# Two tiles of an encoder kernel grow by 32 bytes, and the tiles behind them move in SBUF

## The chip, the core and the metric

The kernel runs on one core of a Trainium2 chip. The metric is the device time of one execution in microseconds (us). Three runs of the kernel before took 1504.77, 1505.03 and 1505.45 us.

## The reference

One encoder layer on 256 tokens of width 2048, float32: an rmsnorm, a combined input projection, windowed and dilated attention, two gated branch projections, an output projection, a gated MLP with a depthwise convolution of width 3, and a gated per-layer embedding. Cut to its products:

```python
proj = rms_norm(x, attn_norm) @ w_in                 # q, k, v, two gates
ya, yb = windowed_gqa(...), dilated_attention(...)
merged = sigmoid(ga) * (ya @ w_branch_a) + sigmoid(gb) * (yb @ w_branch_b)
x = x + merged @ w_out
hf = rms_norm(x, ffn_norm)
x = x + (gelu(dwconv(hf @ w_ffn_gate)) * (hf @ w_ffn_up)) @ w_ffn_down
x = x + sigmoid(rms_norm(x, ple_norm) @ w_ple_gate) * (p @ w_ple_proj)
return rms_norm(x, final_norm)
```

## The kernel before

Tokens lie along the free dimension and features on the 128 partitions. Every weight matrix is cut into blocks of 128x128, and all blocks come in one stream, in the order in which they are used: `load` (L168) brings 16 blocks at a time (1 MB) into one of three `raw` tiles, and `split_to` (L178) turns 8 blocks at a time into two tiles, `whi` (L187, ScalarE, rounded to float32r) and `wlo` (L188, VectorE, the remainder). The activations are split in the same way: a tile such as `mov` holds 256 columns of high parts and then 256 of low parts for each of its 16 chunks of features.

A product takes two matmuls for each block (`block`, L192): the high weights are the stationary operand for 512 moving columns (L198), and the low weights for the 256 high columns (L199). This text calls the two a **pair**. 64 pairs at the start write `first`, and 3552 write `acc`. Two other forms take three matmuls for a step: `value_product` (L241, lines L253 to L255) with 256 moving columns, and `wide_product` (L211, lines L220 to L222) with 512. In these two forms the weights are the moving operand and the activations (`mov`, or `pw`) the stationary one.

The order of the work is written out in `_plan` (L62) as a list of jobs, and TensorE follows it:

- the keys, queries and values, with attention between them: `scores` and `values` (three matmuls, L435 to L437, on `kf`, `qf`, `near` and `v`), and transposes against `ident` (L489);
- 16 rounds of gates and branches: two gates of 16 pairs each from `mov`, then a branch of 8 and one of 4 pairs from `yab`; the first two rounds have gates alone, and two rounds of branches alone end the stage;
- the output projection (16 jobs of 16 pairs from `mov`, kind `o`);
- twice: gates and ups of the MLP (kinds `g` and `u`, 44 jobs of 16 pairs from `mov`), then its down product (kinds `d0` and `d1`, 16 jobs of 22 pairs from `act`). Between the jobs of `d1` the residual is transposed (L638);
- the embedding: `wide_product` on `pw` (kind `pp`, 8 steps) and on `mov` (kind `pg`, 64 steps).

Tiles come from pools that are laid one behind another in SBUF, each tile padded to a multiple of 32 bytes per partition. So a tile's place follows from the sizes ahead of it. The pool `const` (L136) holds `x`, `cl`, `ident`, `ones`, `mhalf` and `warm`; behind it lie `wpool` (`raw`, `whi`, `wlo`), `big` (the two tiles `mov`), `sc` (`tot`, `tb`, `sq`, `t` and others), and then `att`, or later `ff`. `cl` takes 992 bytes, which is 32 bytes more than a multiple of 64, and so what stands behind it is 32 bytes off a multiple of 64; `warm` (16 bytes padded to 32) sets the place of `wpool` and `big`, and `tb` (80 bytes padded to 96) that of all that comes after it. In the programs the places, modulo 64 bytes, are:

| tiles | before | after |
|---|---|---|
| `x`, `cl` | 0 | 0 |
| `ident`, `ones` | 32 | 32 |
| `raw`, `whi`, `wlo` | 32 | 0 |
| `mov` (both), `tot` | 32 | 0 |
| `t`, `u`, `sq`, `rms` and the other wide tiles of `sc` | 0 | 0 |
| `yab`, `near`, `s`, `k`, `kf`, `q`, `qf`, `v`, `vf`, `far` | 0 | 0 |
| `act`, `pw`, `ph`, `c`, `gw` | 0 | 0 |

The slices that the matmuls read start at multiples of 512 bytes within their tiles, so each operand has its tile's remainder. (`value_product` also reads every second token of `mov`, which starts 0 or 4 bytes further on.)

Of the kernel before, what the change touches and what calls it, by code (L numbers as in the profile page):

```python
# [10 lines left out]
F32 = mybir.dt.float32  # L11
FR = mybir.dt.float32r
AF = mybir.ActivationFunctionType
# [3 lines left out]
P = 128  # L17
# [10 lines left out]
NH = QH + BH  # L28
NBUCK = 32
# [103 lines left out]
def _encoder(ctx: ExitStack, tc, xt, pt, cols, table, onehot, mask, ident_in, last_gain, wts, out):  # L133
    nc = tc.nc

    const = ctx.enter_context(tc.tile_pool(name="const", bufs=1))  # L136
# [10 lines left out]
    nc.vector.memset(ones, 1.0)  # L147
    mhalf = const.tile([P, 4], F32, name="mhalf")
    nc.vector.memset(mhalf, -0.5)
    warm = const.tile([P, 4], F32, name="warm")  # L150
    nc.scalar.activation(warm, mhalf, AF.Tanh)
    idle = ps.tile([P, P], F32, name="misc")
    for _ in range(WARM):
        nc.tensor.matmul(idle, ones, ones, start=True, stop=True)
# [106 lines left out]
    sc = ctx.enter_context(tc.tile_pool(name="sc", bufs=2))  # L261
# [95 lines left out]
    hba = hb[:, :QH * AW].rearrange("p (h c) -> p h c", c=AW)  # L357
    hbb = hb[:, QH * AW:].rearrange("p (h c) -> p h c", c=BW)
    oh = ap_.tile([NBUCK, 2 * T], F32, name="oh", tag="near", bufs=1)
    tb = sc.tile([NBUCK, NH], F32, name="tb", bufs=1)  # L360
    mk = ap_.tile([NH, 2 * T], F32, name="mk", tag="s1", bufs=2)
    squares = ap_.tile([P, 4, T], F32, name="squares", tag="s3", bufs=1)

# [427 lines left out]
```

## Time and profile before

| what | value |
|---|---|
| median of three runs | 1505.03 us |
| the profiled execution | 1504.69 us |
| its span in the profile | 1502.9 us |
| VectorE busy | 1051.7 us (70%) |
| ScalarE busy | 765.6 us (51%) |
| DMA, mean | 187 GB/s |

The span runs from the first to the last instruction in the profile; the other 1.8 us of the execution lie around it. In a group of instructions "x2656" is their count and the last number before the bar is the mean duration of one. Matmuls overlap, so the duration of one (394 ns for 512 columns) is longer than the time from one start to the next, which is what sets the pace. In the windows, "(x694)" counts the instructions that touch a stretch of time.

### The profile page before, as it was taken

To read this page: it belongs to the slowest core of one execution; us is meant where nothing else is said; L and a number is where in the kernel's file an instruction comes from. 1 tells how busy PE (TensorE), PEld (TensorE's weight loads), DVE (VectorE), ACT (ScalarE), POOL (GpSimd) and SP (SyncE) were. 2 spreads that over 40 slices of the span, in tenths; PEclk is the share of its full clock that TensorE was granted. 3 is DMA by queue.
4 is the path that set the end of the run, shared out by engine and by line. 5 is a ranking of instruction groups with operands and counts; after the bars stand their busy time and mean duration, and the time that the engine had idled before them with its cause. 6 is when DMAs were issued, how large, how long until landed. Compare 5 with 4: busy or idle time off the path is not lost.

```text
span 1502.9 us, 22107 instructions
## 1 busy us (share of the span) xinstructions
PE 1487.2 (99%) x8680; PEld 1307.7 (87%) x8680; DVE 1051.7 (70%) x1626; ACT 765.6 (51%) x1179; POOL 33.1 (2%) x36
## 2 busy tenths in 40 slices
PE   9999999999999999999999999999999999999996
PEld 7999999988888888888888888888888888888885
DVE  8786665666666677678888885557888887656564
ACT  6564444445555555554555554444555555555543
POOL 7000000000000000000000000000000000000000
PEclk9999999999999999999999999999999999999999
DMA  7744455445555555565555555555555555555552
GB/s 263 278 141 169 168 172 186 160 170 184 194 196 180 188 194 191 182 222 182 186 193 196 188 181 192 196 182 184 195 196 185 184 192 196 176 189 174 190 196 84
DMA packets 43651, 280.95 MB, mean 187 GB/s; under 512 B 4820, under 2 KB 7892, under 8 KB 10908
## 3 DMA queue, kind: packets, MB, share of 16 engines
q1 hardware_dynamic: 42972, 277.45, 52.4%
q10 hardware_dynamic: 576, 2.10, 0.4%
q8 instruction: 68, 1.11, 0.3%
q14 instruction: 35, 0.29, 0.1%
HBM read 277.39 MB, written 2.14 MB: 186 GB/s over the span
## 4 chain that ended last, share of the span: by engine, by line
PE 97%; DVE 1%; DMA 1%; issue 0%; SPq 0%; ACT 0%; DVEq 0%; POOLq 0%; POOL 0%; ACTq 0%
PE acc L198 55%; PE acc L199 28%; PE acc L220 2%; PE acc L222 2%; PE acc L221 2%; PE acc L253 2%; PE acc L255 2%; PE acc L254 2%; DMA raw<-in_wts 1%; PE pt L489 0%; DVE mov L285 0%; DVE wlo L188 0%; PE misc L638 0%; PE misc L504 0%; PE sp L454 0%
## 5 line engine op out<-in xcount | busy, mean ns | idle before, releaser
L198 PE MATMUL acc<-mov,whi 128*128 128x512 f32 x2656 | 928.5, 394 | 0.0
L188 DVE TENSOR_TENSOR wlo<-raw,whi 128x1024 fp32r<-128x1024 f32 (+1 forms) x517 | 635.9, 1230 | 405.4 <-ACT whi L187 405.1
L187 ACT ACTIVATE whi<-raw 128x1024 fp32r<-128x1024 f32 (+1 forms) x517 | 547.3, 1059 | 642.7 <-PE acc L198 390.6
L199 PE MATMUL acc<-mov,wlo 128*128 128x256 f32 x2656 | 741.7, 279 | 0.0
L198 PEld LDWEIGHTS acc<-mov,whi 128*128 128x128 f32 x2656 | 497.6, 187 | 112.2 <-DVE mov L280 0.3
L199 PEld LDWEIGHTS acc<-mov,wlo 128*128 128x128 f32 x2656 | 500.9, 189 | 0.1
L198 PE MATMUL acc<-act,whi 128*128 128x512 f32 x704 | 247.5, 394 | 0.0
L199 PE MATMUL acc<-act,wlo 128*128 128x256 f32 x704 | 196.5, 279 | 0.0
L198 PEld LDWEIGHTS acc<-act,whi 128*128 128x128 f32 x704 | 131.9, 187 | 31.3
L199 PEld LDWEIGHTS acc<-act,wlo 128*128 128x128 f32 x704 | 132.0, 187 | 0.0
L268 ACT ACTIVATE t<-acc 128x256 f32<-128x256 f32 x230 | 84.2, 369 | 22.9 <-PE acc L199 22.9
L272 DVE TENSOR_TENSOR u<-acc,t 128x256 f32<-128x256 f32 x197 | 81.5, 417 | 2.1 <-ACT t L268 2.1
L198 PE MATMUL acc<-yab,whi 128*128 128x512 f32 x192 | 68.4, 396 | 0.0
L253 PE MATMUL acc<-whi,mov 128*128 128x256 f32 x224 | 63.5, 284 | 0.0
L255 PE MATMUL acc<-whi,mov 128*128 128x256 f32 x224 | 63.4, 283 | 0.0
L254 PE MATMUL acc<-wlo,mov 128*128 128x256 f32 x224 | 63.3, 283 | 0.0
L199 PE MATMUL acc<-yab,wlo 128*128 128x256 f32 x192 | 53.9, 281 | 0.0
L220 PE MATMUL acc<-whi,mov 128*128 128x512 f32 x128 | 49.9, 390 | 0.0
L222 PE MATMUL acc<-whi,mov 128*128 128x512 f32 x128 | 49.8, 389 | 0.0
L221 PE MATMUL acc<-wlo,mov 128*128 128x512 f32 x128 | 49.8, 389 | 0.0
L253 PEld LDWEIGHTS acc<-whi,mov 128*128 128x128 f32 x224 | 43.3, 194 | 1.1 <-ACT whi L187 0.8
L198 PEld LDWEIGHTS acc<-yab,whi 128*128 128x128 f32 x192 | 36.0, 188 | 8.8
(143 smaller groups left out, 1034.3 us busy)
## 6 DMA issues: line engine op xcount, KB each, us to landing
raw<-in_wts SPq DMA_DIRECT2D x254, 1024.0 KB, 4.8
raw<-in_wts SPq DMA_DIRECT2D x7, 512.0 KB, 8.1
x<-in_xt SPq DMA_DIRECT2D x7, 256.0 KB, 7.6
mov<-hold SPq DMA_DIRECT2D x3, 514.0 KB, 7.6
mov<-hold SPq DMA_DIRECT2D x2, 768.0 KB, 7.1
mov<-in_last_gain ACTq DMA_DIRECT2D x1, 1024.0 KB
out<-mov SPq DMA_DIRECT2D x2, 384.0 KB, 2.5
out<-mov ACTq DMA_DIRECT2D x2, 384.0 KB, 3.2
```

Of the source, the lines that this page charges most:

```text
L187: nc.scalar.activation(hi, src, AF.Copy)
L188: nc.vector.tensor_tensor(lo, src, hi.bitcast(F32), op=ALU.subtract)
L198: nc.tensor.matmul(acc, hi[:, o, :], m, start=first, stop=False, skip_group_check=True)
L199: nc.tensor.matmul(acc[:, T:], lo[:, o, :], m[:, :T], start=False, stop=last, skip_group_check=True)
L220: nc.tensor.matmul(accs[t], xh, hi, start=(k == 0), stop=False)
L221: nc.tensor.matmul(accs[t], xh, lo, start=False, stop=False)
L222: nc.tensor.matmul(accs[t], xl, hi, start=False, stop=(k == n - 1))
L253: nc.tensor.matmul(acc[:, :T], xh, hi, start=(k == 0), stop=False)
L254: nc.tensor.matmul(acc[:, :T], xh, lo, start=False, stop=False)
L255: nc.tensor.matmul(acc[:, :T], xl, hi, start=False, stop=(k == KC - 1))
L268: keep(nc.scalar.activation(t, acc[:, T:], AF.Copy, scale=scale))
L272: nc.vector.tensor_tensor(u, acc[:, :T], t, op=ALU.add)
```

## The change

`warm` gets 12 columns in place of 4, of which the same four are written. `tb` gets 28 columns in place of 20, of which the same 20 are used. Both tiles take 32 bytes more per partition, so `wpool` and `big` move by 32 bytes, and what lies behind `tb` by 64. Every instruction is the same on every engine, in the same order and with the same waits; only addresses differ.

```diff
-    warm = const.tile([P, 4], F32, name="warm")
-    nc.scalar.activation(warm, mhalf, AF.Tanh)
+    warm = const.tile([P, 12], F32, name="warm")
+    nc.scalar.activation(warm[:, :4], mhalf, AF.Tanh)
...
-    tb = sc.tile([NBUCK, NH], F32, name="tb", bufs=1)
+    tb = sc.tile([NBUCK, NH + 8], F32, name="tb", bufs=1)[:, :NH]
```

## The prediction, made before the run

> **What bounds the kernel now.** I read the first page first, for the engine that is never idle, and then the chain of work that ended last.
>
> ```profile
> span 1502.9 us, 22107 instructions
> PE 1487.2 (99%) x8680; PEld 1307.7 (87%) x8680; DVE 1051.7 (70%) x1626; ACT 765.6 (51%) x1179; POOL 33.1 (2%) x36
> PEclk9999999999999999999999999999999999999999
> PE 97%; DVE 1%; DMA 1%; issue 0%; SPq 0%; ACT 0%; DVEq 0%; POOLq 0%; POOL 0%; ACTq 0%
> L198 PE MATMUL acc<-mov,whi 128*128 128x512 f32 x2656 | 928.5, 394 | 0.0
> L199 PE MATMUL acc<-mov,wlo 128*128 128x256 f32 x2656 | 741.7, 279 | 0.0
> L198 PE MATMUL acc<-act,whi 128*128 128x512 f32 x704 | 247.5, 394 | 0.0
> L198 PE MATMUL acc<-yab,whi 128*128 128x512 f32 x192 | 68.4, 396 | 0.0
> L220 PE MATMUL acc<-whi,mov 128*128 128x512 f32 x128 | 49.9, 390 | 0.0
> ```
>
> TensorE is 99% busy, its clock is at full speed in every slice, and 97% of the chain is its own work: the end is set by how closely matmuls follow each other. The mean durations say nothing of that (394 ns from `mov` and from `act` alike), because matmuls overlap. So I counted matmuls in long stretches that hold nothing but pairs of one kind: the output projection (from `mov`), the first gates and ups (`mov`), the first down product (`act`), the second gates and ups (`mov`).
>
> ```profile
> core 0: us, PE busy (x), PEclk, DMA share, GB/s
> 899.00:1019.00 120.00, 120.00 (x688) 1.00 0.53 185
> 1025.00:1145.00 120.00, 120.00 (x694) 1.00 0.54 191
> ...
> 700.00:820.00 120.00, 120.00 (x694) 1.00 0.54 191
> 568.00:652.00 84.00, 84.00 (x477) 1.00 0.54 190
> ```
>
> A count takes in matmuls already under way (0.33 us of them, about the mean duration of one), so the time of a pair is twice (stretch + 0.33) / count. That gives 346.8 ns for gates and ups, **349.8 ns from `act`**, and 353.6 ns in the output projection, though all four have the same shapes, the same engine clock and no idle time. There are three rhythms here. `mov` is read in two of them, so it has a good one and a bad one; `act` has one in between. (A pair has 768 columns.) By the table of places, `mov` with `whi` and `wlo` are all at 32 modulo 64, while `act` is at 0 and its weights at 32.
>
> The embedding product shows the same more sharply, in two jobs that take turns. Both stream the same weights tile (at 32); the stationary operand is `pw` (at 0) or `mov` (at 32).
>
> ```profile
> 1401.47 0.40 PE L221 MATMUL acc<-wlo,pw 128*128 128x512 f32 x1
> ...
> 1403.82 0.40 PE L222 MATMUL acc<-whi,pw 128*128 128x512 f32 x1
> ...
> 1404.28 0.39 PE L220 MATMUL acc<-whi,mov 128*128 128x512 f32 x1
> ...
> 1405.87 0.39 PE L221 MATMUL acc<-wlo,mov 128*128 128x512 f32 x1
> ```
>
> From `pw`, ten matmuls lie between the two starts: 2.35 / 10 = 235 ns each. From `mov` there are seven: 1.59 / 7 = 227 ns. So the pace is lower where the two operands of a matmul have different remainders, whichever of them is at 0.
>
> Does 0 on both sides occur? Yes, at 256 columns: the scores' triples (`kf` and `qf`, both at 0) stand beside the value products, both operands at 32.
>
> ```profile
> 56.88 0.28 PE L435 MATMUL sp<-kf,qf 128*128 128x256 f32 x1
> ...
> 57.48 0.28 PE L437 MATMUL sp<-kf,qf 128*128 128x256 f32 x1
> 57.59 0.39 PE L198 MATMUL acc<-mov,whi 128*128 128x512 f32 x1
> ...
> 175.80 0.28 PE L254 MATMUL acc<-wlo,mov 128*128 128x256 f32 x1
> ...
> 177.35 0.28 PE L255 MATMUL acc<-whi,mov 128*128 128x256 f32 x1
> ```
>
> Six triples' matmuls take 0.71 us (118 ns each); thirteen of the value product take 1.55 us (119 ns each). Both at 0 is no better and no worse than both at 32. My reading: it is the difference of the two remainders that costs, not the remainder.
>
> **The change part by part.** No instruction is added, taken away or reordered, and no wait changes. What changes is which pairs of operands differ. By the table, all matmuls from `mov` go from both at 32 to both at 0, which by the reading above costs nothing. Three groups go from unlike to alike:
>
> 1. The down products, 704 pairs from `act`: from 349.8 to 346.8 ns, 3.0 x 704 = 2.1 us saved.
> 2. The branch products, 192 pairs from `yab`. They are short runs between gates, so I price whole rounds. The chain has a mark of 0.26 us, the same matmul of each round's first branch job:
>
> ```profile
> 350.28 0.26 PE acc L198
> ...
> 549.79 0.26 PE acc L198
> ```
>
>    There are 13 rounds between these two marks, 199.51 / 13 = 15.347 us for a round of 32 + 12 = 44 pairs. At 346.8 ns these take 15.259 us. Saved: 0.088 us a round, and for 16 rounds 1.4 us.
> 3. The embedding from `pw`, 16 steps by three matmuls (8 steps for each half): 48 x (235 - 227) = 0.4 us.
>
> The sum is 3.9 us, all of it on the chain, since TensorE never waits in these stages. Transposes against `ident` keep unlike remainders (`ident` stays at 32), so "all operands" is not quite met, and I expect nothing of them.
>
> The other engines and the queues read and write moved tiles too:
>
> ```profile
> L280 DVE TENSOR_TENSOR act<-u,act 128x256 fp32r<-128x256 f32 x44 | 18.4, 418 | 0.0
> L280 DVE TENSOR_TENSOR mov<-mb,mov 128x256 fp32r<-128x256 f32 x16 | 6.7, 418 | 0.0
> x<-in_xt SPq DMA_DIRECT2D x7, 256.0 KB, 7.6
> raw<-in_wts SPq DMA_DIRECT2D x2, 256.0 KB, 3.7
> ```
>
> The same VectorE line takes 418 ns into `act` (at 0) and into `mov` (at 32): nothing, and TensorE's work covers it anyway. For DMAs there is no fair pair. Loads of 256 KB into `x` (at 0) took longer than those into `raw` (at 32), but stood in a fuller queue, so they speak for no gain. The chain gives DMA 1%, 15 us, nearly all at the start where TensorE waits for the first weights. If the place changed a transfer by 5%, an estimate for both sides, that would be 0.7 us either way. I take zero.
>
> The profiled execution took 1504.69 us, and 1504.69 - 3.9 = 1500.8. The median of the runs before is 0.3 us above the profiled execution, so I forecast **1501.1 us** for the median after.
>
> One rule speaks against this. The Trainium skill, "TensorE: Matmul & The Clock Gate", in "Part 2: What happens when you issue a matmul", says that the stationary load has a read port of its own and takes nothing from the running matmul; by that the two operands' places could not disturb each other. The rows from `pw` and `mov` (235 and 227 ns under the same stream) do not agree with it for this kernel.
>
> **The rivals.**
>
> *Nothing changes.* The slower stages are slow for another reason: `act`, `yab` and `pw` all lie behind `tb`, at the far end of SBUF, and their stages have their own neighbours on VectorE and ScalarE. Then moving them by 64 bytes leaves each rhythm where it is, and the time is 1505.0 us. For it: remainder and region cannot be told apart in these rows. Against it: the output projection's `mov` is the slowest of all, lies nearer and has no unlike remainder, so region alone orders the stages wrongly. The Trainium skill, "SBUF — State Buffer", in "Specifications (TRN2)", gives lines of 16 bytes; 32 and 64 are both multiples of that, and by that page this rival holds. No row here shows a line's width.
>
> *Offset 0 itself is dear (slower).* The 512-column matmuls in this profile with an operand at 0 are slower than the usual rhythm of those at 32. If that is a cost of the place and not of the difference, the 2656 pairs from `mov` all take the 349.8 ns of `act`: 2400 of them lose 3.0 ns (7.2 us), and the 256 of the output projection gain 3.8 (1.0 us). The wide matmuls from `mov` (x128 on each of three lines, 384) then take the 235 ns of `pw`, and 8 x 384 = 3.1 us is lost. Together 9.3 us: 1505.0 + 9.3 = 1514.3 us. It decides as soon as 512 columns at 0 meet weights at 0, a case that the trace doesn't hold. Against it: the 256-column triples at 0 and 0 are not slow.
>
> *The bad rhythm spreads (slower, or a smaller gain).* The 353.6 ns of the output projection began after a wait and held for the whole stage; stages with unlike remainders return to 349.8 after every disturbance. With all alike, a stage can be caught in the bad rhythm and keep it. The price is 6.8 ns a pair. In the second down product alone (352 pairs, disturbed by transposes) that takes back 2.4 us; over the second gates, ups and down product (704 + 352 in the worst case) it is 7.2 us, and 1501.1 + 7.2 = 1508.3 us. The other way, a good rhythm in the output projection saves 256 x 6.8 = 1.7 us more, which gives 1499.4.
>
> *Both at 0 is better than both at 32.* A pair takes 346.8 ns; if whatever is lost between matmuls halved, an estimate of 13 ns a pair from the spread of the rhythms (twice 6.8), 3616 pairs would save 47 us: 1458 us. The triples at 118 ns against 119 speak plainly against it.
>
> **How the numbers follow.** The forecast, with rhythms that fall well or badly in one stage (1498 to 1503.5): 0.55. Nothing changes: 0.20. Offset 0 dear: 0.15. The bad rhythm in more than a stage: 0.07. Both at 0 better: 0.03. A measurement of this kernel tells about 0.2%, 3.0 us, from no change. The forecast lies 3.9 us below, so about a tenth of its cases end within 0.2%. Faster: 0.49 + 0.03 = 0.52. Same: 0.20 + 0.06 + 0.01 = 0.27. Slower: 0.15 + 0.06 = 0.21. The range from 1497 to 1510 leaves out most of the dear offset and the great gain, and holds the DMA's 0.7 us at both ends. The likeliest case by itself has 1498 to 1503.5.
>
> **What would show it.** In 120 us of the first down product, 694 matmuls in place of 688 show step 1 right; 688 show that nothing changed. The marks of 0.26 us should be gone and a round take 15.26 us (step 2). `pw`'s matmuls should start every 227 ns (step 3). Gates and ups must still count 694; 688 there is the dear offset, 680 the bad rhythm, and over 700 a gain that I don't expect. Wrong would be, above all, the step from the triples of 256 columns to 512: no row shows both operands at 0 for the pair.

## The result and the profile after

| | before | after |
|---|---|---|
| median (lowest to highest) | 1505.24 us (1504.77 to 1508.19) | 1513.70 us (1513.59 to 1514.31) |
| profiled execution, span | 1504.69, 1502.9 us | 1514.31, 1512.5 us |

After divided by before is 1.0054, with a 95% interval of 1.0043 to 1.0066: the change makes the kernel 0.5% **slower**. I had forecast 1501.1 us and a range up to 1510.

On its page the kernel after is bound by TensorE at full clock, as before. The mean duration of the wide matmuls (512 columns) from `mov` has grown from 394 to 397 ns; that of the wide ones from `act` has not, while their narrow ones (256 columns) went from 279 to 283 ns.

```profile
span 1512.5 us, 22107 instructions
PE 1495.1 (99%) x8680; PEld 1311.2 (87%) x8680; DVE 1051.9 (70%) x1626; ACT 765.6 (51%) x1179; POOL 32.9 (2%) x36
PEclk9999999999999999999999999999999999999999
PE 97%; DVE 1%; DMA 1%; issue 0%; SPq 0%; ACT 0%; DVEq 0%; POOLq 0%; POOL 0%; ACTq 0%
L198 PE MATMUL acc<-mov,whi 128*128 128x512 f32 x2656 | 937.5, 397 | 0.0
L198 PE MATMUL acc<-act,whi 128*128 128x512 f32 x704 | 248.1, 394 | 0.0
L199 PE MATMUL acc<-act,wlo 128*128 128x256 f32 x704 | 199.1, 283 | 0.0
```

The counts of matmuls in stretches of the kernel after, in this order: the first down product, the second gates and ups, the first gates and ups, the output projection. (Counts in brackets, as before.)

```profile
903.00:1023.00 120.00, 120.00 (x686) 1.00 0.52 185
1040.00:1160.00 120.00, 120.00 (x681) 1.00 0.52 186
700.00:820.00 120.00, 120.00 (x694) 1.00 0.54 192
570.50:654.50 84.00, 84.00 (x477) 1.00 0.53 191
```

The down product was to rise from 688 to 694; it fell to 686 (350.8 ns a pair; before, 349.8). The first gates and ups kept their 694 with both operands at 0. The second ones fell from 694 to 681, which is 353.4 ns a pair: the bad rhythm that only the output projection had shown so long before. The starts of the stages in the two timelines tell where the 9.6 us of span lie:

| from, to | before, us | after, us | difference |
|---|---|---|---|
| start, first branch product | 349.4 | 351.6 | 2.2 |
| branch rounds | 212.2 | 214.4 | 2.2 |
| output projection | 90.6 | 90.6 | 0.0 |
| first gates and ups | 245.0 | 245.0 | 0.0 |
| first down product | 123.2 | 123.6 | 0.4 |
| second gates and ups | 244.1 | 248.8 | 4.7 |
| second down product to the end | 238.4 | 238.5 | 0.1 |

Of the first 2.2 us, 0.5 are there already at the first value product (L253 starts at 35.16 and at 35.65 us); the other 1.7 lie in the keys, queries and values.

The chain of the kernel after now marks one long matmul after another in the gates of the rounds:

```profile
372.24 0.24 PE acc L198
373.30 0.24 PE acc L198
374.36 0.24 PE acc L198
```

They are 1.06 us apart, which is three pairs at 353.3 ns. The bad rhythm goes round in three pairs: by the trace's starts to the nanosecond, its three wide matmuls are followed after 232, 241 and 235 ns. Before, every wide matmul of the same gates was followed after 230 ns, and three pairs took 1.04 us, without such marks:

```profile
372.14 0.39 PE L198 MATMUL acc<-mov,whi 128*128 128x512 f32 x1
...
373.18 0.39 PE L198 MATMUL acc<-mov,whi 128*128 128x512 f32 x1
```

### The profile page after: what moved, and what is told of

Read it like the earlier page. It is cut to its first block, busy times and chain, and to the rows that moved or that the text cites. A ratio compares the mean times of both kernels' runs of the same rounds, so it can differ in the third digit from the quotient of the medians.

```text
span 1512.5 us, 22107 instructions
## 1 busy us (share of the span) xinstructions
PE 1495.1 (99%) x8680; PEld 1311.2 (87%) x8680; DVE 1051.9 (70%) x1626; ACT 765.6 (51%) x1179; POOL 32.9 (2%) x36
## 4 chain that ended last, share of the span: by engine, by line
PE 97%; DVE 1%; DMA 1%; issue 0%; SPq 0%; ACT 0%; DVEq 0%; POOLq 0%; POOL 0%; ACTq 0%
PE acc L198 55%; PE acc L199 28%; PE acc L220 2%; PE acc L222 2%; PE acc L221 2%; PE acc L253 2%; PE acc L255 2%; PE acc L254 2%; DMA raw<-in_wts 1%; DVE mov L285 0%; PE pt L489 0%; DVE wlo L188 0%; PE misc L638 0%; PE sp L454 0%; PE misc L504 0%
## 5 line engine op out<-in xcount | busy, mean ns | idle before, releaser
L253 PE MATMUL acc<-whi,mov 128*128 128x256 f32 x224 | 63.5, 284 | 0.0
L253 PEld LDWEIGHTS acc<-whi,mov 128*128 128x128 f32 x224 | 43.3, 194 | 1.1 <-ACT whi L187 0.8
L254 PEld LDWEIGHTS acc<-wlo,mov 128*128 128x128 f32 x224 | 43.4, 194 | 0.0
```

The costliest lines, as they stand in the source:

```text
L253: nc.tensor.matmul(acc[:, :T], xh, hi, start=(k == 0), stop=False)
L254: nc.tensor.matmul(acc[:, :T], xh, lo, start=False, stop=False)
```

## The experiments

**Which move does it?** My reading (remainders modulo 64) was wrong at first sight, since `act` and its weights have like remainders after and are no faster. Theory A took its place: the distance between weights and `act` sets the rhythm of down and branch products, and the gates behind them fall into a rhythm that hangs on it and that they keep. Its rivals were the offset 0 itself (B) and chance (C). Modulo 256 the distance is 96 before and 128 after. Two kernels make one half of the change each, a third moves all tiles behind `const` by 64 bytes, and a fourth puts `act` and `yab` at a multiple of 512 from the weights, as `mov` is.

```diff
 e1:  warm [P, 4]  -> [P, 12]
 e2:  tb [NBUCK, NH] -> [NBUCK, NH + 8]
 e3:  warm [P, 4]  -> [P, 20]
 e4:  tb [NBUCK, NH] -> [NBUCK, NH + 44]
```

> Only warm grows: weights and mov go to offset 0 modulo 64, act and yab to 32, and the distance from the weights to act stays what it was before (352 modulo 512). Theory A (the rhythm in which the down and branch products run decides the rhythm that the gates after them fall into, and it hangs on the distance between the operands): as before, 1505 us, 694 matmuls in 120 us of the second gates and ups. Theory B (mov and weights at 0 are prone to the slow rhythm): as after, 1513 to 1514 us, 681 matmuls. Theory C (any shift of places throws the rhythms anew): some other time, not predictable.

Measured 1504.57 us; ratio to before 0.9998 (0.9989 to 1.0007).

> Only tb grows: weights and mov stay at 32 modulo 64, act and yab go to 32 as well, and the distance from the weights to act becomes that of after (384 modulo 512). Theory A: as after, 1513 to 1514 us, act at 351 ns a pair, gates after it at 353.6. Theory B: as before, 1505 us. Theory C: not predictable.

Measured 1514.08 us; ratio 1.0059 (1.0042 to 1.0076). The counts of e1, then of e2, for the first down product and the second gates and ups:

```profile
905.00:1019.00 114.00, 114.00 (x653) 1.00 0.52 186
1040.00:1160.00 120.00, 120.00 (x694) 1.00 0.54 193
```

```profile
905.00:1019.00 114.00, 114.00 (x651) 1.00 0.53 186
1040.00:1160.00 120.00, 120.00 (x681) 1.00 0.52 185
```

Weights and `mov` at 0 cost nothing (e1), so B is out. The whole loss comes with the second tile, where weights and `mov` stay at 32 (e2).

> warm grows by 64 bytes: all tiles behind it move by 64, so every remainder modulo 64 and every distance between weights, mov, act and yab stays as before; only x, cl, ident and ones stay put. Theories A and B: as before, 1505 us within 0.1%. Theory C: another time, by up to 8 us.

Measured 1504.83 us; ratio 1.0000 (0.9990 to 1.0009). Moving is harmless as long as the distances stay, which is against C.

> tb grows to 256 bytes: weights and mov stay as before (32 modulo 64), act and yab lie at a distance from the weights that is a multiple of 512, as mov does. If the rhythm of a product hangs on that distance modulo 512, the down and branch products take 346.8 or 353.6 ns a pair like mov, no longer 349.8 or 351: 1501 us if the good rhythm holds all through, up to 1520 us if the slow one is caught and kept from the gates on. If the distance plays no part, 350 or 351 ns remain and the time is 1505 or 1513 us.

Measured 1514.52 us; ratio 1.0062 (1.0047 to 1.0077). In its timeline the branch products run at `mov`'s good rhythm (346.7 ns); then the first gates and ups fall into the bad one, and the down product behind them and the second gates keep it. Down product, second and first gates of e4:

```profile
905.00:1019.00 114.00, 114.00 (x647) 1.00 0.53 188
1040.00:1160.00 120.00, 120.00 (x681) 1.00 0.52 186
700.00:820.00 120.00, 120.00 (x681) 1.00 0.52 185
```

So the rhythms go with the distance: at a multiple of 512 `act` has those of `mov`. And the bad one, once caught, stays for over 1700 pairs, to the first transposes of the second down product.

> tb grows to 512 bytes: act and yab lie at a distance from the weights that is a multiple of 256 but not of 512; all else as in the kernel with the multiple of 512. If the period is 256 bytes or less, the down and branch products have mov's rhythms (346.8 or 353.6 ns) as at 512; if it is 512 or more they have another one, such as 350 or 351 ns. The time follows from the rhythms that are caught, 1501 to 1520 us.

Measured 1513.78 us (1.0058, 1.0036 to 1.0080; two executions), with the rhythms of e4 in every stage. A distance of 768 does what 512 does, so at these two the period is 256 or a part of it.

**Is the rhythm a state?** Four transposes that nothing reads are set between two blocks of a gate job. They interrupt the stream, and which rhythm follows is called a throw here, good or bad. In e5 and e6 they stand in the second job of the second gates, in the kernel after and in the one before.

```diff
+    def idle_turn():
+        p = ps.tile([P, 2, 2, P], F32, name="misc")
+        for t in range(2):
+            for c in range(2):
+                nc.tensor.transpose(p[:, t, c, :], ident, ident)
...
+        if kind == "g" and n == FHALF:
+            at((i + 1, 4), idle_turn)
```

> The kernel after, with four idle transposes (ident against ident, result never read) set into the second job of the second gates and ups; nothing else differs. Theory A (the slow rhythm is a state that a stage keeps until it is disturbed): the rhythm is thrown anew at that point. If it comes out good, some 680 pairs run at 346.8 ns in place of 353.6, 4.6 us less, the transposes cost about 0.6 us, and the time is 1509.5 to 1510 us; if it comes out slow again, 1514.3 us. If the slow rhythm belongs to the places of the tiles (theory B), it must come back at once: 1514.3 us and 681 matmuls in 120 us.

Measured 1509.93 us (1.0032, 1.0018 to 1.0046), as foretold.

> The kernel before with the same four idle transposes at the same point, where its rhythm is the good one. Theory A: the transposes cost 0.6 us if the good rhythm comes back (1505.5 us), and if the throw comes out slow, some 680 pairs lose 6.8 ns each (1510 us). Without a kept state: 1505.5 us and 694 matmuls in 120 us.

Measured 1510.17 us (1.0034, 1.0022 to 1.0047), as foretold for a bad throw. The second gates of e5, then of e6:

```profile
1040.00:1160.00 120.00, 120.00 (x694) 1.00 0.54 193
```

```profile
1040.00:1160.00 120.00, 120.00 (x681) 1.00 0.52 185
```

The same 0.36 us disturbance turns the bad rhythm into the good one in the kernel after, and the good into the bad in the kernel before. The places of the tiles cannot hold the rhythm; it is a state of the stream of matmuls. The timeline of e5 around the transposes (start, duration, engine, line):

```profile
1031.63 0.40 PE L198 MATMUL acc<-mov,whi 128*128 128x512 f32 x1
1031.87 0.28 PE L199 MATMUL acc<-mov,wlo 128*128 128x256 f32 x1
1031.98 0.40 PE L198 MATMUL acc<-mov,whi 128*128 128x512 f32 x1
...
1032.34 0.60 PE L646 MATMUL misc<-ident 128*128 128x128 f32 x4
1032.69 0.48 PE L198 MATMUL acc<-mov,whi 128*128 128x512 f32 x1
...
1033.47 0.39 PE L198 MATMUL acc<-mov,whi 128*128 128x512 f32 x1
1033.70 0.28 PE L199 MATMUL acc<-mov,wlo 128*128 128x256 f32 x1
1033.82 0.39 PE L198 MATMUL acc<-mov,whi 128*128 128x512 f32 x1
```

Ahead of them a wide matmul is followed after 0.24 us (233, 241 and 236 ns in turn), behind them after 0.23 us (230 ns each). The mean of the three is 6.7 ns longer, and that is the whole difference.

**Can the throw be steered?** In e4's profile the branch rounds and the output projection are good and the first gates and ups are not, so one good throw there should gain 11 us. The same transposes were put there (e7: fourth job, ahead of block 4), twice (e9: fourth and fifth job), with two transposes instead of four (e10), and ahead of blocks 5 and 6 (e11, e12).

> The kernel with act and yab at a multiple of 512 from the weights, with the same idle transposes in the fourth job of the first gates and ups, where it had fallen into the slow rhythm. Theory A: if the throw comes out good, all pairs from there to the transposes of the second down product run at 346.8 ns: 656 + 352 + 704 pairs by 6.8 ns, 11.6 us less than without them, and 1503 us; with one more good stage in the second down product down to 1501. If it comes out slow: 1515 us.

> act and yab at a multiple of 512 from the weights, and idle transposes in the fourth and again in the fifth job of the first gates and ups. One such disturbance left the slow rhythm slow; in the second down product of the same layout a second one in a row made it good. Theory A: if the second throw comes out good, 640 + 352 + 704 pairs gain 6.8 ns each, 11.5 us against 1513.8 us, and the time is 1502 to 1503 us; if it comes out slow, 1514.5 us. If the slow rhythm belonged to the place of the tiles, 1514.5 us.

> The same layout with a shorter disturbance, two idle transposes in the fourth job of the first gates and ups. Theory A: another length is another throw; good gives 1502 to 1503 us, slow 1513.8 us, and nothing between, since the rhythm is kept from there to the second down product.

> The layout with act and yab at a multiple of 512, the four idle transposes one block later than before (ahead of block 5 in place of block 4 of the same job). The slow rhythm goes round in three pairs, whose wide matmuls take 233, 241 and 236 ns. The four throws that came out slow in this layout interrupted it behind a 236 or a 241; the throw that came out good (in the kernel after) interrupted it behind a 233. Theory A, made sharper (the place in the round at which it is interrupted decides): block 5 is interrupted behind a 233, the throw comes out good, and some 655 + 352 + 704 pairs gain 6.8 ns: 1502 to 1503 us, 694 matmuls in 120 us of both gates and ups and of the first down product. If the throw were chance, or the layout were slow by its places: 1514 us.

> The same with the idle transposes ahead of block 6: the round is interrupted behind a 241. Theory A, made sharper: slow, 1514 to 1515 us. If any throw at another place than block 4 came out good: 1502 to 1503 us.

Measured 1513.82, 1514.55, 1515.79, 1514.88 and 1513.97 us: every throw came out bad. In e11 the rhythm was interrupted where the sharper form of theory A wanted it (behind the shortest of the three steps, 232 ns), and the throw was bad all the same, so that form fell.

What decides a throw stays open, and two things in these traces bound it. It is not mere chance: behind the transposes of the residual, the eight stretches of e4's second down product ran at 353.3, 353.3, 346.7, 346.7, 353.3, 353.3, 346.7 and 346.7 ns a pair, and those of e7, e8, e9 and e12 did so in the same order (e10 and e11 differ in one stretch each). Nor is it the addresses alone: up to the first gates e11 has the instructions and addresses of e4, and yet its output projection fell into the bad rhythm and e4's into the good one. The counts of e4, then of e11:

```profile
570.50:654.50 84.00, 84.00 (x487) 1.00 0.55 194
```

```profile
570.50:654.50 84.00, 84.00 (x478) 1.00 0.54 192
```

**Does the distance decide?** Only `tb` grows: by 20, 28, 36, 52 and 60 columns, for the distances 160, 192, 224, 32 and 64 modulo 256.

> Only tb grows, so that act and yab lie 160 bytes modulo 256 from the weights (before: 96, after: 128). Theory D (that distance alone sets the rhythm of the down and branch products, and through it which rhythm the gates after them fall into): a rhythm of its own, neither 346.8 nor 353.6 ns, the same in both down products, and the gates after all branch jobs and the second gates all alike, either all good (1502 to 1506 us) or all slow (1512 to 1515 us). Rival (each entry is thrown anew): gates after the 14 branch rounds come out mixed within one run.

> Distance 192 modulo 256, both at 32 modulo 64, so with like remainders. Theory D: as for 160, gates all alike, 1502 to 1506 us or 1512 to 1515 us. If like remainders modulo 64 made the throw bad (as at 128), slow: 1512 to 1515 us.

> Distance 224 modulo 256, unlike remainders modulo 64. Theory D: as for 160, gates all alike. If unlike remainders made the throw good (as at 96), good: 1502 to 1506 us.

> Distance 32 modulo 256, unlike remainders modulo 64. Theory D: as for 160, gates all alike. If unlike remainders made the throw good (as at 96), good: 1502 to 1506 us.

> Only tb grows, distance 64 modulo 256, the last multiple of 32 that was not tried. Theory D: one rhythm in both down products and all gates behind branches alike; 1500 to 1506 us if these gates are good, 1512 to 1516 us if they are slow. Like remainders at 128 and 192 were followed by slow gates; by that rule slow.

All distances in one table, pairs from the counts (in brackets) of the first down product (905 to 1019 us) and of the second gates (1040 to 1160 us). One count more or less is about 0.5 ns:

| distance modulo 256 | down, ns a pair | gates behind it, ns | time, us |
|---|---|---|---|
| 0 (e4, e8) | 353.4 (x647), kept | 353.4 (x681), kept | 1514.52, 1513.78 |
| 32 (e16) | 346.5 (x660) | 346.8 (x694) | 1502.15 |
| 64 (e18) | 349.1 (x655) | 346.8 (x694) | 1505.29 |
| 96 (before) | 350.2 (x653) | 347.3 (x693) | 1505.24 |
| 128 (after) | 351.2 (x651, e2) | 353.4 (x681) | 1513.70 |
| 160 (e13) | 346.5 (x660) | 353.4 (x681) | 1507.44 |
| 192 (e14) | 352.9 (x648) | 353.4 (x681) | 1514.85 |
| 224 (e15) | 353.4 (x647) | 346.3 (x695) | 1512.99 |

The lines of e13, then of e15:

```profile
905.00:1019.00 114.00, 114.00 (x660) 1.00 0.54 188
1040.00:1160.00 120.00, 120.00 (x681) 1.00 0.53 186
```

```profile
905.00:1019.00 114.00, 114.00 (x647) 1.00 0.52 185
1040.00:1160.00 120.00, 120.00 (x695) 1.00 0.53 187
```

Both change with the distance, and one does not follow from the other: 160 has the best down product and bad gates behind it. Like remainders modulo 64 (0, 64, 128, 192) are neither good nor bad. Within a run the 13 stretches of gates between the branch products were alike at 32, 96, 128, 160, 192 and 224. But the distance does not fix everything: at 64 the first of these stretches was bad and the other 12 good, and six of the eight stretches of its second down product ran at about 353 ns, not 349; at 224 one of those eight ran at 346.7 ns. So the history counts too. At 224 the first gates had fallen into the bad rhythm as well, which is most of its loss.

Several expectations missed. Theory D put e13 at 1502 to 1506 or at 1512 to 1515 us and gave its down product a rhythm of its own; it took 1507.44 us, its down product had the pace of the good rhythm, and its gates were bad. Unlike remainders did not bring e15 to 1502 to 1506 us, and the rule that slow gates follow like remainders, tried again in e18, fell.

All tiles behind `tb` move along with `act` and `yab`, also those that only VectorE and ScalarE use. They do not make the pace of the down product: by the starts in the traces, its pairs took 346.7 ns in e16, 353.3 ns in e14 and 349.9 and 350.1 ns before, the same within 0.2 ns while these two engines worked on other tiles than `whi` and `wlo` and while they did not.

Distance 32 beats both kernels: ratio to before 0.9982 (0.9971 to 0.9993). The first down product, second and first gates of e16:

```profile
905.00:1019.00 114.00, 114.00 (x660) 1.00 0.54 193
1040.00:1160.00 120.00, 120.00 (x694) 1.00 0.53 190
700.00:820.00 120.00, 120.00 (x695) 1.00 0.55 193
```

The last kernel takes the whole change, weights and `mov` at 0, and only sets the distance to 32.

```diff
-    tb = sc.tile([NBUCK, NH + 8], F32, name="tb", bufs=1)[:, :NH]
+    tb = sc.tile([NBUCK, NH + 52], F32, name="tb", bufs=1)[:, :NH]
```

> The kernel after (weights and mov at 0 modulo 64) with a larger tb, so that act and yab lie 32 bytes modulo 256 from the weights instead of 128. Theory D (the distance modulo 256 decides, not the remainder modulo 64): as with distance 32 and weights at 32, good gates behind the branches and in both halves of the MLP, down products at 346.7 ns a pair, 1501 to 1503 us. If the remainder of weights and mov mattered beside it: slower, up to 1513 us.

Measured 1501.83 us; ratio to before 0.9977 (0.9967 to 0.9986). Its counts are those of e16:

```profile
905.00:1019.00 114.00, 114.00 (x660) 1.00 0.54 190
1040.00:1160.00 120.00, 120.00 (x694) 1.00 0.54 192
700.00:820.00 120.00, 120.00 (x695) 1.00 0.55 192
```

The same change of weights and `mov` takes 1501.8 us with one distance behind it and 1513.7 us with another.

## Why the prediction was wrong

- *What bounds the kernel* held: TensorE's pace and nothing else. The DMAs and VectorE stayed out of it, as costed.
- **The first step that failed** is "it is the difference of the two remainders that costs". The rows were right, the period was not. Remainder modulo 64 and distance modulo 256 cannot be told apart in the profile of before, where one distance (96) stands beside one other (0). I took the smaller number because the change spoke of it. With like remainders at 128, `act` got slower, 350.8 for 349.8 ns a pair.
- *Steps 1 and 2* (2.1 and 1.4 us saved): the first down product lost 0.4 us. By the starts in the traces the branch products did gain, 0.4 us, while the gates between them lost 2.6 us, so the rounds as a whole lost 2.2.
- *Step 3* (0.4 us): half right. From `pw`, the timeline of after has eight matmuls between these starts, 231 ns each, in place of 235; 227 was forecast.

```profile
1405.05 0.39 PE L220 MATMUL acc<-whi,pw 128*128 128x512 f32 x1
...
1406.90 0.40 PE L222 MATMUL acc<-whi,pw 128*128 128x512 f32 x1
```

- **The second step that failed, and the dearer one,** is that all matmuls from `mov` "go from both at 32 to both at 0", which "costs nothing". The second gates and ups lost 4.7 us and the gates of the branch rounds 2.6 us. Their own operands kept their distance; what changed was the rhythm of the product ahead of them, and so the state in which they began. The prediction had seen that a stage keeps its rhythm, and had not asked what the stage before hands over.
- *Rival "offset 0 is dear"* named 1514.3 us, close to 1513.7, by a mechanism that did not take place: at 0 the first gates still count 694, and e1 takes 1504.57 us. A right number is no proof of a cause.
- *Rival "the bad rhythm spreads"* came nearest to the mechanism, with 0.07 too little a chance. Its price of 6.8 ns a pair held; its base (a gain of 3.9 us) and its extent did not, since the bad rhythm also took the branch rounds and part of the queries. Its condition, like remainders, was not what let it in: at distance 160, with unlike ones, the gates were bad too. Nor do stages with unlike remainders return to 349.8 ns after every disturbance: before, the eight stretches of the second down product ran at 350.0 to 351.2 ns.
- *Rival "nothing changes"* had each rhythm stay where `act` is moved; in the eight layouts the first down product ran at 346.5 to 353.4 ns. By the lines of 16 bytes in the Trainium skill, "SBUF — State Buffer", "Specifications (TRN2)", places that differ by 32 bytes would be alike. e16 and e18 differ by 32 bytes in the place of `act`, and by 3 us.
- By the rule of the Trainium skill, "TensorE: Matmul & The Clock Gate", "Part 2: What happens when you issue a matmul", that the stationary load takes nothing from the running matmul, how far the two operands lie apart should not matter. These runs do not agree: e1 and e2 have the same instructions and differ in this distance, and by 9.5 us. Whether it is the load that disturbs the running matmul, and where in the chip the two would meet, no run here shows.

Open are what decides which rhythm follows a disturbance, why the queries and the output projection fell as they did in each layout, and whether the period is 256 for all distances.

## What to carry to other kernels

When a kernel is bound by back-to-back matmuls, count matmuls in long stretches of one kind before looking for a cause: equal shapes with unequal counts show a loss that busy time, waits and mean durations hide. A change of layout, even by 32 bytes, then has to be measured over several paddings, since one padding says little about its neighbour: in this kernel nine sizes of one small tile gave 1502 to 1515 us. What a stage costs can depend on the stage before it, so compare stage by stage and not by sums.

## What the runs showed of the hardware

A stream of float32r matmuls with 512 and 256 columns in turn ran here at 346.7 or at 353.3 ns a pair with the same operands, the same clock and no wait, and kept its rhythm for over 1700 pairs. A disturbance of 0.36 us can change the one into the other in both directions. The pace also changes with the distance between stationary and moving operand in SBUF: in the first down product it ran from 346.5 to 353.4 ns a pair over the eight multiples of 32 bytes modulo 256. What came before in the stream counts beside it.
